# One inverse square root chain for each token tile of queries and keys, in place of four

## The chip, the cores and the metric

One core of a Trainium2 chip runs the whole program in one launch. The engines are named as in the profile: PE is TensorE (matmuls and transposes; PEld are its weight loads), DVE is VectorE, ACT is ScalarE, POOL is GpSimd, and SP issues most of the DMAs. The metric is the device time of the program in microseconds (us), lower being better; the median of several runs is given. All arithmetic is in float32, and a matmul of full precision is made of three products of high and low parts.

## The reference

The reference is one encoder layer over two sequences of 1024 and 256 tokens, taken here as 1280 tokens, or 10 tiles of 128. Only this part is touched: queries and keys of 8 heads are normalised head by head before the rotary embedding and the attention.

```python
q = (rms_norm(c_q, q_a_norm) @ w_uq).reshape(bsz, seq, N_HEADS, QK_HEAD)      # 96 per head
kv = (rms_norm(c_kv, kv_a_norm) @ w_ukv).reshape(bsz, seq, N_HEADS, QK_NOPE + V_HEAD)
k = jnp.concatenate([k_nope, k_rope], axis=-1)     # k_rope is shared by the heads
q = rms_norm(q, q_head_norm)       # x * rsqrt(mean(x*x) + EPS) * g, over the 96 of a head
k = rms_norm(k, k_head_norm)
...                                # rotary embedding on the last 32, then softmax attention
```

So each token has 8 inverse square roots for its queries and 8 for its keys. The rest of the layer (modulation, a convolution branch, a gated branch, three sigmoid gates, output products, a feed-forward block) is untouched.

## The kernel before

The program is one long list of jobs. 36 of them are products with a block of the input weights (`in_job`, 72 matmuls of `mm3` at L139 into a big PSUM tile); the last 24 of these make the gates (`gate`, L592 and L593: sigmoid on ACT, a store of 640 KB by SP). Smaller pieces of work wait in a list called `side`, and `run_side(n)` between two jobs takes n of them. Their instructions then stand in the program behind the gate just done and ahead of the next.

Queries and keys are such pieces (`prep_steps`). A token tile i has four units, in this order: queries of heads 0 to 3 (`q_unit`, tile psq), keys and values of heads 0 to 3 (`kv_unit`, tile pskv), then both for heads 4 to 7. One step makes one unit; four steps follow each of the gates 4 to 15, so that a gate and the four units of one tile make a turn. There are 40 units in 10 turns, and 12 turns have room for 48 steps.

A unit goes like this. PE makes the products (L510 or L535) into a PSUM tile. ACT squares them into a working slot `b_` (L513, L538). DVE sums the squares for each of 4 heads (L515, L540), scales the 4 sums (L516, L541), and runs `rsqrt_small` on the 4 columns: two integer instructions (L158, L159) and three rounds of three (L162 to L164), all on 128x4 tiles named zq or zk; a last instruction (L519, L544) folds in another factor. That is 13 small instructions a unit besides the sum. DVE also multiplies the products out of PSUM into `b_` (L524, three times, or L546), and POOL multiplies `b_` by the roots (L526 for queries, L550 and L548 for the two halves of the keys). For values ACT and DVE make a high and a low part (L555, L556), and SP stores them (L558).

`flip` comes LAG = 3 steps later: PE transposes the four heads of `b_` into a PSUM tile (L495), ACT copies it into a slot `o` (L497), DVE makes the low part (L498), and SP stores both halves, 256 KB each, to qk_d (L500). So step j issues unit j and then the flip of unit j - 3. The attention reads qk_d later, through POOL's queue.

Three resources are shared. psq, pskv and the transposes' tile pt take turns on two PSUM buffers (pool `sm`), so that each matmul of these kinds waits until the tile two before it has been read out. `b_`, `o`, the values' slot `vo`, the loaded latents and the gates take slots from one list of 33, of which the oldest free one is always used next; a slot that a DMA stores from is written again only when that DMA has landed. While the units run, 22 of the slots are held throughout (16 with the split activations h, 4 with split weights, 2 with tables). In the list as the program works it, 4 slots are free at the tightest place, and a slot is used again 5 to 7 takes after it was dropped. The weight blocks of a gate are split on POOL (L117, whi) and DVE (L120, wlo) one block at a time, when the buffers of an earlier block come free.

The order of each engine's instructions is fixed when the program is built, by a planner with costs of its own. It is not the order of the source: an instruction whose inputs are late by the plan steps behind later ones. So matmuls of the next gate stand between the matmuls of two units, and instructions of two units alternate on DVE. On the chip each engine keeps that order and waits where an input comes later than planned.

Of the kernel before, what the change touches and what calls it, by code (L numbers as in the profile page):

```python
# [11 lines left out]
F32 = mybir.dt.float32  # L12
# [3 lines left out]
ALU = mybir.AluOpType  # L16
AX = mybir.AxisListType
# [3 lines left out]
P = 128  # L21
# [6 lines left out]
EPS = 1e-6  # L28
# [6 lines left out]
LAG = 3  # L35
# [46 lines left out]
def build(tc, A):  # L82
# [6 lines left out]
    sm_p = enter(tc.tile_pool(name="smalls", bufs=4))  # L89
# [3 lines left out]
    V, S, G, PE, SY = nc.vector, nc.scalar, nc.gpsimd, nc.tensor, nc.sync  # L93
# [63 lines left out]
    def rsqrt_small(y, s, t):  # L157
        V.tensor_scalar(out=y.bitcast(I32), in0=s.bitcast(I32), scalar1=1, scalar2=None, op0=ALU.arith_shift_right)  # L158
        V.tensor_scalar(out=y.bitcast(I32), in0=y.bitcast(I32), scalar1=-1, scalar2=0x5F3759DF,  # L159
                        op0=ALU.mult, op1=ALU.add)  # L160
        for _ in range(3):
            V.scalar_tensor_tensor(out=t, in0=y, scalar=-0.5, in1=y, op0=ALU.mult, op1=ALU.mult)  # L162
            V.tensor_tensor(out=t, in0=t, in1=s, op=ALU.mult)
            V.scalar_tensor_tensor(out=y, in0=t, scalar=1.5, in1=y, op0=ALU.add, op1=ALU.mult)  # L164
# [25 lines left out]
    for k in range(KD):  # L190
# [3 lines left out]
        sq = sl.take()  # L194
# [3 lines left out]
    ps = big.tile([P, 1536], F32, name="pb", tag="pb")  # L198
# [5 lines left out]
    h = []  # L204
# [287 lines left out]
    def flip(src, which, i, g):  # L492
# [8 lines left out]
                         o[:, p * 512:(p + 1) * 512].bitcast(F32).rearrange("f (h t) -> f h t", h=4))  # L501
        sl.drop(o)

    def q_unit(i, g):
        ps = sm.tile([P, 512], F32, name="psq", tag="sm")
        for k in range(2):
            lh, ll = lat_of(i, k)
            wh, wl = kept[k]
            for q, (a, b) in enumerate(((lh, wh), (lh, wl), (ll, wh))):
                PE.matmul(ps[:, :384], a, b[:, g * 384:(g + 1) * 384], start=k == 0 and q == 0, stop=k == 1 and q == 2)  # L510
        b_ = sl.take()
        sq = b_[:, 512:896]
        S.activation(out=sq, in_=ps[:, :384], func=AF.Square)  # L513
        z = sm_p.tile([P, 4, 4], F32, name="zq", tag="z")
        V.tensor_reduce(out=z[:, 0, :], in_=sq.rearrange("p (h d) -> p h d", h=4), axis=AX.X, op=ALU.add)  # L515
        V.tensor_scalar(out=z[:, 0, :], in0=z[:, 0, :], scalar1=rr[:, 4, i:i + 1], scalar2=EPS,  # L516
                        op0=ALU.mult, op1=ALU.add)
        rsqrt_small(z[:, 1, :], z[:, 0, :], z[:, 2, :])
        V.tensor_scalar(out=z[:, 1, :], in0=z[:, 1, :], scalar1=rr[:, 2, i:i + 1], scalar2=96.0 ** -0.5,  # L519
                        op0=ALU.mult, op1=ALU.mult)  # L520
        qs = b_[:, :512].rearrange("p (h d) -> p h d", h=4)
        pv = ps[:, :384].rearrange("p (h d) -> p h d", h=4)
        for o, a, n in ((0, 0, 96), (96, 80, 16), (112, 64, 16)):
            V.tensor_tensor(out=qs[:, :, o:o + n], in0=pv[:, :, a:a + n],  # L524
                            in1=kept["cs"][:, i, o:o + n].unsqueeze(1).to_broadcast([P, 4, n]), op=ALU.mult)
        G.tensor_tensor(out=qs, in0=qs, in1=z[:, 1, :].unsqueeze(2).to_broadcast([P, 4, P]), op=ALU.mult)  # L526
        return b_, 0, i, g

    def kv_unit(i, g):
        gq, kr = kept["gq"], kept["kr"]  # L530
        ps = sm.tile([P, 512], F32, name="pskv", tag="sm")
        lh, ll = lat_of(i, 2)
        wh, wl = kept[g]
        for q, (a, b) in enumerate(((lh, wh), (lh, wl), (ll, wh))):
            PE.matmul(ps, a, b[:, 768:1280], start=q == 0, stop=q == 2)  # L535
        b_ = sl.take()
        sq = b_[:, 512:768]
        S.activation(out=sq, in_=ps[:, :256], func=AF.Square)  # L538
        z = sm_p.tile([P, 4, 4], F32, name="zk", tag="z")
        V.tensor_reduce(out=z[:, 0, :], in_=sq.rearrange("p (h d) -> p h d", h=4), axis=AX.X, op=ALU.add)  # L540
        V.tensor_scalar(out=z[:, 0, :], in0=z[:, 0, :], scalar1=rr[:, 5, i:i + 1], scalar2=rr[:, 6, i:i + 1],  # L541
                        op0=ALU.mult, op1=ALU.add)
        rsqrt_small(z[:, 1, :], z[:, 0, :], z[:, 2, :])
        V.tensor_scalar(out=z[:, 2, :], in0=z[:, 1, :], scalar1=rr[:, 3, i:i + 1], scalar2=None, op0=ALU.mult)  # L544
        ks = b_[:, :512].rearrange("p (h d) -> p h d", h=4)
        V.tensor_tensor(out=ks[:, :, 0:64], in0=ps[:, :256].rearrange("p (h d) -> p h d", h=4),  # L546
                        in1=gq[:, 96:160].unsqueeze(1).to_broadcast([P, 4, 64]), op=ALU.mult)
        G.tensor_tensor(out=ks[:, :, 0:64], in0=ks[:, :, 0:64],  # L548
                        in1=z[:, 2, :].unsqueeze(2).to_broadcast([P, 4, 64]), op=ALU.mult)
        G.tensor_tensor(out=ks[:, :, 64:128], in0=kr[:, i, :].unsqueeze(1).to_broadcast([P, 4, 64]),  # L550
                        in1=z[:, 1, :].unsqueeze(2).to_broadcast([P, 4, 64]), op=ALU.mult)
        vo = sl.take(F32R)
        vv = vo[:, :512].rearrange("p (h t d) -> p h t d", h=4, t=2)
        vp = ps[:, 256:512].rearrange("p (h d) -> p h d", h=4)
        S.activation(out=vv[:, :, 0, :], in_=vp, func=AF.Copy, scale=rr[:, 3, i:i + 1])  # L555
        V.scalar_tensor_tensor(out=vv[:, :, 1, :], in0=vp, scalar=rr[:, 3, i:i + 1],  # L556
                               in1=vv[:, :, 0, :].bitcast(F32), op0=ALU.mult, op1=ALU.subtract)
        SY.dma_start(v_d[g * 4:g * 4 + 4, :, i, :].rearrange("h p d -> p h d"),  # L558
                     vo[:, :512].bitcast(F32).rearrange("p (h d) -> p h d", h=4))
        sl.drop(vo)  # L560
        return b_, 1, i, g

    def prep_steps():
        units = [(i, g, f) for i in range(NT) for g in range(2) for f in (q_unit, kv_unit)]
        wait = []

        def step(j):
            if j < len(units):
                i, g, f = units[j]
                if (i, 0) == (0, g) and f is q_unit:  # L570
                    lat_get(0)
                if g == 0 and f is kv_unit and i + 1 < NT:
                    lat_get(i + 1)
                wait.append(f(i, g))
                if g == 1 and f is kv_unit:
                    sl.drop(kept.pop(("lat", i)))
            if j >= LAG:
                b_, which, i, g = wait.pop(0)
                flip(b_, which, i, g)
                sl.drop(b_)  # L580
            if j == len(units) + LAG - 1:
                for k in range(2):
                    sl.drop(*kept.pop(k))
                sl.drop(kept.pop("csg"), kept.pop("krr"))

        for j in range(len(units) + LAG):
            side.append(lambda j=j: step(j))

    def gate(br, m):
# [660 lines left out]
```

## Time and profile before

| | us |
|---|---|
| median of 3 runs | 2191.18 (2187.65 to 2191.96) |
| the profiled execution, its time | 2189.91 |
| the profiled execution, its span | 2188.1 |
| PE busy in the span | 2088.0 (95%) |
| DVE busy | 1541.6 (70%) |
| ACT busy | 750.9 (34%) |
| POOL busy | 688.7 (31%) |

The units' matmuls lie between 424.5 and 627 us from the start of the span, the flips between 433.8 and 640.6. The gates go on until 768 us, where the attention begins. A timeline row gives the start, the length, the engine, the line, the operation with what it writes and reads, and in brackets the engine's idle time ahead of it with what ended that. A busy PE is not PE at its peak, since ends of matmuls are modelled: successive matmuls overlap in the rows.

### The profile page before, as it was taken

Reading aid. Unit: us, or ns where it says so; the run is one execution under the profiler, and the core shown is the slowest. Engines: PE = TensorE matmul, PEld = TensorE weight load, DVE = VectorE, ACT = ScalarE, POOL = GpSimd, SP = SyncE. Lnnn points to the kernel's source line nnn. Section 1 sums busy time; section 2 is a strip of 40 time slices with the busy share of each in tenths; the row PEclk is TensorE's granted clock in tenths of the full one; section 3 lists DMA queues with packets and bytes.
Section 4 is the critical chain, followed back from the end, with each engine's and each line's share of the span. In section 5 each row is a group of like instructions: output and inputs, shape, how many; then the busy total and the mean of one; then the engine's idle time right before and its main releaser. Section 6 shows DMA issues by size and latency. Waiting matters only on the chain. (4 is left out here: it accounts for less than half of the span.)

```text
span 2188.1 us, 30072 instructions
## 1 busy us (share of the span) xinstructions
PE 2088.0 (95%) x11264; PEld 1791.5 (82%) x11264; DVE 1541.6 (70%) x2530; ACT 750.9 (34%) x1273; POOL 688.7 (31%) x541
## 2 busy tenths in 40 slices
PE   5899999999999999999999996999999999899999
PEld 5688888877778878888888875888888888688889
DVE  7696788778776778887796398766676666744344
ACT  5210031122322277763000155544444444322223
POOL 3401301322221234452043454444443444511000
PEclk9999999999999999999999998999999999999999
DMA  7301213366674723336635321223223232646455
GB/s 266 114 13 53 101 72 115 110 194 199 203 257 148 270 90 121 121 109 221 227 137 194 107 96 61 94 90 99 87 82 95 89 101 98 229 167 203 131 168 164
DMA packets 146546, 300.86 MB, mean 137 GB/s; under 512 B 12128, under 2 KB 69600, under 8 KB 146400
## 3 DMA queue, kind: packets, MB, share of 16 engines
q1 hardware_dynamic: 136032, 254.37, 34.6%
q0 software_dynamic: 10368, 44.57, 6.6%
q8 instruction: 89, 1.46, 0.3%
q14 instruction: 57, 0.47, 0.1%
HBM read 220.24 MB, written 78.64 MB: 137 GB/s over the span
## 5 line engine op out<-in xcount | busy, mean ns | idle before, releaser
L1033 PE MATMUL b<-t,wq 128*128 128x512 f32 (+1 forms) x2904 | 550.8, 352 | 18.9 <-ACT t L1055 13.1
L1033 PEld LDWEIGHTS b<-t,wq 128*128 128x128 f32 x2904 | 474.4, 190 | 95.7 <-ACT t L1055 13.6
L139 PE MATMUL pb<-t,whi 128*128 128x512 f32 (+1 forms) x1728 | 471.1, 358 | 8.1 <-DVE t L120 7.6
L120 DVE TENSOR_TENSOR wq<-wst,wq 128x512 fp32r<-128x512 f32 x308 | 252.2, 826 | 200.8 <-ACT wq L938 199.8
L139 PEld LDWEIGHTS pb<-t,whi 128*128 128x128 f32 x1728 | 307.1, 190 | 54.9 <-DVE t L120 9.3
L938 ACT ACTIVATE wq<-wst 128x512 fp32r<-128x512 f32 x308 | 193.1, 630 | 378.5 <-PE pd L1157 164.6
L1157 PE MATMUL pd<-t,wq 128*128 128x512 f32 (+1 forms) x1584 | 307.3, 356 | 10.4 <-ACT wq L938 5.0
L139 PE MATMUL pb<-t,wlo 128*128 128x512 f32 (+1 forms) x864 | 309.3, 358 | 1.6 <-DVE wlo L120 1.6
L1157 PEld LDWEIGHTS pd<-t,wq 128*128 128x128 f32 x1584 | 263.9, 191 | 53.8 <-ACT wq L938 5.4
L117 POOL TENSOR_SCALAR whi<-wst 128x1024 fp32r<-128x1024 f32 (+1 forms) x76 | 100.6, 1325 | 392.8 <-PE pb L139 207.1
L117 POOL TENSOR_SCALAR t<-t 128x512 fp32r<-128x512 f32 (+5 forms) x94 | 116.1, 1243 | 326.1 <-DMA t<-act_d 183.7
L139 PE MATMUL bp<-t,whi 128*128 128x512 f32 x640 | 198.9, 391 | 2.9 <-DVE t L120 2.9
L281 DVE SCALAR_TENSOR_TENSOR t<-t,col,t 128x1009 f32<-128x1009 f32 (+14 forms) x240 | 193.8, 871 | 0.0
L120 DVE TENSOR_TENSOR t<-t,t 128x512 fp32r<-128x512 f32 (+4 forms) x130 | 137.1, 1082 | 77.1 <-POOL t L117 76.2
L139 PEld LDWEIGHTS pb<-t,wlo 128*128 128x128 f32 x864 | 163.8, 190 | 23.5 <-DVE wlo L120 2.0
L120 DVE TENSOR_TENSOR wlo<-wst,whi 128x1024 fp32r<-128x1024 f32 (+1 forms) x76 | 86.0, 1134 | 98.5 <-POOL whi L117 63.1
L139 PEld LDWEIGHTS bp<-t,whi 128*128 128x128 f32 x640 | 118.1, 188 | 27.2 <-DVE t L120 4.1
L139 PE MATMUL bp<-t,wlo 128*128 128x512 f32 x320 | 124.5, 389 | 0.0
L693 POOL TENSOR_SCALAR t<-t,sz 128x1024 f32<-128x1024 f32 (+1 forms) x80 | 82.0, 1025 | 121.2 <-DVE sz L692 106.8
L685 PE MATMUL ps<-t,t 128*128 128x512 f32 (+1 forms) x432 | 114.5, 398 | 4.0 <-ACT t L691 2.5
L1091 POOL TENSOR_TENSOR t<-t,t 128x1280 f32<-128x1280 f32 x22 | 72.7, 3305 | 122.9 <-ACT wq L938 109.9
L592 ACT ACTIVATE t<-pb 128x1280 f32<-128x1280 f32 x24 | 29.8, 1242 | 209.6 <-PE pb L139 204.4
(199 smaller groups left out, 2902.1 us busy)
## 6 DMA issues: line engine op xcount, KB each, us to landing
wst<-in_wup SPq DMA_DIRECT2D x66, 512.0 KB, 3.6
wst<-in_wdn SPq DMA_DIRECT2D x132, 256.0 KB, 2.8
t<-in_ada SPq DMA_DIRECT2D x48, 512.0 KB, 5.7
qk_d<-t SPq DMA_DIRECT2D x80, 256.0 KB, 3.1
t<-qk_d POOLq DMA_DIRECT2D x32, 640.0 KB, 5.0
wst<-in_win SPq DMA_DIRECT2D x36, 512.0 KB, 3.8
gate_d<-t SPq DMA_DIRECT2D x24, 640.0 KB, 3.1
t<-gate_d SPq DMA_DIRECT2D x24, 640.0 KB, 5.5
```

The costliest lines, as they stand in the source:

```text
L117: G.tensor_scalar(out=out, in0=in_, scalar1=1.0, scalar2=0.0, op0=ALU.mult, op1=ALU.add)
L120: V.tensor_tensor(out=out, in0=in_, in1=hi.bitcast(F32), op=ALU.subtract)
L139: PE.matmul(ps.at(o, n) if isinstance(ps, Two) else ps[:, o:o + n], ws[:, c:c + P], ms[:, s:s + n], start=first and j == 0 and q == 0, sto ...
L281: V.scalar_tensor_tensor(out=ac[:, o + a:o + e], in0=ci[:, o + a + d:o + e + d], scalar=w, in1=ac[:, o + a:o + e], op0=ALU.mult, op1=ALU.add)
L592: S.activation(out=gt, in_=ps[:, :T], func=AF.Sigmoid)
L685: PE.matmul(ps[:, o + c:o + c + w], qk[a][:, q0:q0 + P], qk[b][:, k0 + c:k0 + c + w], start=q == 0, stop=q == 2)
L693: G.tensor_scalar(out=pr[:, o:o + n], in0=pr[:, o:o + n], scalar1=z[:, 2:3], scalar2=0.0, op0=ALU.mult, op1=ALU.add)
L938: S.activation(out=w[:, :HB], in_=src, func=AF.Copy)
L1033: PE.matmul(ps, w[:, c + k * P:c + (k + 1) * P], bs[k][i], start=start and k == 0 and q == 0, stop=stop and k == 3 and q == 2, skip_group_ ...
L1091: G.tensor_tensor(out=c["y1"], in0=c["y1"], in1=y2, op=ALU.mult)
L1157: PE.matmul(pss[m][:, :n], w[:, a + m * P:a + (m + 1) * P], t[:, b:b + n], start=k == 0 and q == 0, stop=k == KF - 1 and q == 2)
```

## The change

The 4 + 4 + 4 + 4 sums of a tile's four units go into one tile zt of 128x3x16. A unit now only squares, multiplies and sums. Behind the fourth unit, `scale_tile` scales the 16 sums with two instructions, runs `rsqrt_small` once on 16 columns, folds in the factors with two instructions, and then POOL multiplies all four units (six instructions). The flips wait for that: unit u of tile i, made in step 4i + u, is flipped in step 4i + u + 5 where it was 4i + u + 3. The last flip is in step 44, and step 45 drops the weights' slots. In `q_unit` the multiplications out of PSUM now stand ahead of the sum. With more `b_` slots held, 2 slots of the list are free at the tightest place, and most are used again 3 to 5 takes after they were dropped.

```diff
+    zt = {}
+
+    def sums(i, c, sq):
+        if c == 0:
+            zt[i] = sm_p.tile([P, 3, 16], F32, name="zt", tag="z")
+        V.tensor_reduce(out=zt[i][:, 0, c:c + 4], in_=sq.rearrange("p (h d) -> p h d", h=4), axis=AX.X, op=ALU.add)
+
     def q_unit(i, g):
...
         S.activation(out=sq, in_=ps[:, :384], func=AF.Square)
-        z = sm_p.tile([P, 4, 4], F32, name="zq", tag="z")
-        V.tensor_reduce(out=z[:, 0, :], in_=sq.rearrange("p (h d) -> p h d", h=4), axis=AX.X, op=ALU.add)
-        V.tensor_scalar(out=z[:, 0, :], in0=z[:, 0, :], scalar1=rr[:, 4, i:i + 1], scalar2=EPS,
-                        op0=ALU.mult, op1=ALU.add)
-        rsqrt_small(z[:, 1, :], z[:, 0, :], z[:, 2, :])
-        V.tensor_scalar(out=z[:, 1, :], in0=z[:, 1, :], scalar1=rr[:, 2, i:i + 1], scalar2=96.0 ** -0.5,
-                        op0=ALU.mult, op1=ALU.mult)
...
-        G.tensor_tensor(out=qs, in0=qs, in1=z[:, 1, :].unsqueeze(2).to_broadcast([P, 4, P]), op=ALU.mult)
+        sums(i, g * 8, sq)
         return b_, 0, i, g
 
     def kv_unit(i, g):
...
+        sums(i, g * 8 + 4, sq)
         SY.dma_start(v_d[g * 4:g * 4 + 4, :, i, :].rearrange("h p d -> p h d"),
...
+    def scale_tile(i, units):
+        z = zt.pop(i)
+        zs = [z[:, r, :].rearrange("p (g f h) -> p g f h", g=2, f=2) for r in range(3)]
+        V.tensor_scalar(out=zs[0][:, :, 0, :], in0=zs[0][:, :, 0, :], scalar1=rr[:, 4, i:i + 1], scalar2=EPS,
+                        op0=ALU.mult, op1=ALU.add)
+        V.tensor_scalar(out=zs[0][:, :, 1, :], in0=zs[0][:, :, 1, :], scalar1=rr[:, 5, i:i + 1],
+                        scalar2=rr[:, 6, i:i + 1], op0=ALU.mult, op1=ALU.add)
+        rsqrt_small(z[:, 1, :], z[:, 0, :], z[:, 2, :])
+        V.tensor_scalar(out=zs[2][:, :, 0, :], in0=zs[1][:, :, 0, :], scalar1=rr[:, 2, i:i + 1], scalar2=96.0 ** -0.5,
+                        op0=ALU.mult, op1=ALU.mult)
+        V.tensor_scalar(out=zs[2][:, :, 1, :], in0=zs[1][:, :, 1, :], scalar1=rr[:, 3, i:i + 1], scalar2=None,
+                        op0=ALU.mult)
+        for b_, f, _, g in units:
+            bs = b_[:, :512].rearrange("p (h d) -> p h d", h=4)
+            w = P if f == 0 else 64
+            G.tensor_tensor(out=bs[:, :, 0:w], in0=bs[:, :, 0:w],
+                            in1=zs[2][:, g, f, :].unsqueeze(2).to_broadcast([P, 4, w]), op=ALU.mult)
+            if f:
+                G.tensor_tensor(out=bs[:, :, 64:128], in0=kept["kr"][:, i, :].unsqueeze(1).to_broadcast([P, 4, 64]),
+                                in1=zs[1][:, g, 1, :].unsqueeze(2).to_broadcast([P, 4, 64]), op=ALU.mult)
...
                 if g == 1 and f is kv_unit:
                     sl.drop(kept.pop(("lat", i)))
-            if j >= LAG:
-                b_, which, i, g = wait.pop(0)
+                    scale_tile(i, wait)
+                    scaled.extend((j + 2, u) for u in wait)
+                    wait.clear()
+            if scaled and scaled[0][0] <= j:
+                b_, which, i, g = scaled.popleft()[1]
                 flip(b_, which, i, g)
                 sl.drop(b_)
```

## Rows read from the trace of the kernel before

**Rows 1.** Windows, turns 2 to 10: busy us (count) of PE, PEld, DVE, ACT, POOL.

```profile
442.85:634.00 191.15, 175.85 (x951) 147.14 (x950) 155.09 (x639) 58.94 (x103) 53.57 (x70) 1.00 0.67 204
```

**Rows 2.** Waits, 420 to 636 us: total us, times, longest.

```profile
PE pskv L535 <- DVE zq L162: 14.8, 9, 1.7
PEld pskv L535 <- issue: 22.4, 18, 2.1
```

**Rows 3.** Timeline of PE: first matmuls of two successive gates with no units between.

```profile
396.97 0.63 PE L139 MATMUL pb<-t,whi 128*128 128x512 f32 x2
...
410.75 0.63 PE L139 MATMUL pb<-t,whi 128*128 128x512 f32 x2
```

**Rows 4.** Timeline of PE: one turn, from its first unit to the next turn's.

```profile
506.93 1.21 PE L510 MATMUL psq<-t,t 128*128 128x384 f32 x6
...
510.92 0.93 PE L535 MATMUL pskv<-t,t 128*128 128x512 f32 x3
...
514.21 1.22 PE L510 MATMUL psq<-t,t 128*128 128x384 f32 x6
...
517.55 0.61 PE L139 MATMUL pb<-t,whi 128*128 128x512 f32 x2
519.83 0.94 PE L535 MATMUL pskv<-t,t 128*128 128x512 f32 x3 [1.66 <-DVE zq L162]
...
528.26 0.34 PE L510 MATMUL psq<-t,t 128*128 128x384 f32 x1
```

**Rows 5.** Timeline of DVE in the same turn.

```profile
508.15 1.23 DVE L120 TENSOR_TENSOR wlo<-wst,whi 128x1024 fp32r<-128x1024 f32 x1 [3.04 <-PE psq L510]
...
515.03 1.04 DVE L163 TENSOR_TENSOR zk<-zk 128x4 f32<-128x4 f32 x1
...
518.18 0.67 DVE L544 TENSOR_SCALAR zk<-zk,rr 128x4 f32<-128x4 f32 x1
...
518.83 0.21 DVE L524 TENSOR_TENSOR t<-psq,t 128x64 f32<-128x64 f32 x1
518.96 0.60 DVE L159 TENSOR_SCALAR zq<-zq 128x4 int32<-128x4 int32 x1
519.47 0.21 DVE L524 TENSOR_TENSOR t<-psq,t 128x64 f32<-128x64 f32 x1
```

**Rows 6.** Timeline of POOL in the same turn.

```profile
507.07 1.04 POOL L117 TENSOR_SCALAR whi<-wst 128x1024 fp32r<-128x1024 f32 x1 [0.34 <-PE pb L139]
515.02 1.04 POOL L526 TENSOR_TENSOR t<-t,zq 128x512 f32<-128x512 f32 x1 [6.90 <-DVE zk L162]
518.21 0.61 POOL L550 TENSOR_TENSOR t<-t,zk 128x256 f32<-128x256 f32 x1 [2.15 <-DVE zk L164]
```

**Rows 7.** Windows, turns 2 to 10, tile zk, then zq: busy us of DVE, POOL.

```profile
442.85:634.00 191.15, 66.19 (x252) 21.64 (x36) 1.00 0.67 204
...
442.85:634.00 191.15, 53.31 (x252) 18.74 (x18) 1.00 0.67 204
```

**Rows 8.** Tiles zq and zk: instructions by line, ns minimum/median/maximum, starts.

```profile
L515 DVE TENSOR_REDUCE zq<-t x20: 544/545/553, 426.9 to 623.5; 128x4 f32<-128x384 f32 x20
...
L163 DVE TENSOR_TENSOR zk<-zk x60: 145/163/1048, 430.9 to 632.3; 128x4 f32<-128x4 f32 x60
...
L540 DVE TENSOR_REDUCE zk<-t x20: 405/420/422, 428.4 to 627.7; 128x4 f32<-128x256 f32 x20
```

**Rows 9.** Tile qk_d, 424 to 640 us: landing of the stores of L500.

```profile
DMA to landing us min/median/max: 2.3/3.0/7.8
```

**Rows 10.** Timeline of ACT: copies of two flips in the turn of Rows 4.

```profile
512.61 0.60 ACT L497 ACTIVATE t<-pt 128x512 fp32r<-128x512 f32 x1 [0.34 <-PE pt L495]
...
515.95 0.60 ACT L497 ACTIVATE t<-pt 128x512 fp32r<-128x512 f32 x1
```

**Rows 11.** Timelines of DVE and ACT: end of side work, last gate's sigmoid.

```profile
751.88 0.23 DVE L614 TENSOR_SCALAR ada<-ada,col 128x2 f32<-128x2 f32 x1
...
766.56 1.24 ACT L592 ACTIVATE t<-pb 128x1280 f32<-128x1280 f32 x1 [12.53 <-PE pb L139]
```

More of the change, by code (lines that the diff above doesn't have):

```diff
@@ L525, in q_unit @@
                             in1=kept["cs"][:, i, o:o + n].unsqueeze(1).to_broadcast([P, 4, n]), op=ALU.mult)
-        G.tensor_tensor(out=qs, in0=qs, in1=z[:, 1, :].unsqueeze(2).to_broadcast([P, 4, P]), op=ALU.mult)
+        sums(i, g * 8, sq)
         return b_, 0, i, g
     def kv_unit(i, g):
-        gq, kr = kept["gq"], kept["kr"]
+        gq = kept["gq"]
         ps = sm.tile([P, 512], F32, name="pskv", tag="sm")
@@ L538, in kv_unit @@
         S.activation(out=sq, in_=ps[:, :256], func=AF.Square)
[L539 to L551, printed above, removed]
         vo = sl.take(F32R)
@@ L555, in kv_unit @@
         S.activation(out=vv[:, :, 0, :], in_=vp, func=AF.Copy, scale=rr[:, 3, i:i + 1])
+        ks = b_[:, :512].rearrange("p (h d) -> p h d", h=4)
+        V.tensor_tensor(out=ks[:, :, 0:64], in0=ps[:, :256].rearrange("p (h d) -> p h d", h=4),
+                        in1=gq[:, 96:160].unsqueeze(1).to_broadcast([P, 4, 64]), op=ALU.mult)
         V.scalar_tensor_tensor(out=vv[:, :, 1, :], in0=vp, scalar=rr[:, 3, i:i + 1],
                                in1=vv[:, :, 0, :].bitcast(F32), op0=ALU.mult, op1=ALU.subtract)
+        sums(i, g * 8 + 4, sq)
         SY.dma_start(v_d[g * 4:g * 4 + 4, :, i, :].rearrange("h p d -> p h d"),
@@ L561, in kv_unit @@
         return b_, 1, i, g
+    def scale_tile(i, units):
[18 more added lines that the diff above has]
+                                in1=zs[1][:, g, 1, :].unsqueeze(2).to_broadcast([P, 4, 64]), op=ALU.mult)
     def prep_steps():
         units = [(i, g, f) for i in range(NT) for g in range(2) for f in (q_unit, kv_unit)]
-        wait = []
+        wait, scaled = [], deque()
+        last = len(units) + LAG + 2
         def step(j):
@@ L576, in step @@
                     sl.drop(kept.pop(("lat", i)))
-            if j >= LAG:
-                b_, which, i, g = wait.pop(0)
+                    scale_tile(i, wait)
[3 more added lines that the diff above has]
+                b_, which, i, g = scaled.popleft()[1]
                 flip(b_, which, i, g)
                 sl.drop(b_)
-            if j == len(units) + LAG - 1:
+            if j == last:
                 for k in range(2):
@@ L584, in step @@
                 sl.drop(kept.pop("csg"), kept.pop("krr"))
-        for j in range(len(units) + LAG):
+        for j in range(last + 1):
             side.append(lambda j=j: step(j))
```

## The prediction

> **What bounds the kernel now.** I read the busy times by stretch first, then the waits of TensorE, then the timelines of one turn (a gate and the four units behind it). Queries and keys fill 191 us, the turns of tiles 1 to 9. In them PE is busy 175.85 us, DVE 155.09, ACT 58.94, POOL 53.57, and the granted clock is 1.00, so PE runs at its upper level throughout [rows 1]. PE is the bound, DVE the next behind it. The list of waits shows one wait of PE of any size there: the keys' products wait 14.8 us for DVE, 9 times, 1.7 at the longest, which is once a turn and 1.65 us each [rows 2]. A gate alone takes 410.75 - 396.97 = 13.78 us [rows 3]; a turn takes 528.26 - 506.93 = 21.33 us [rows 4]; four units and four flips so cost 7.55 us with that stall in them.
>
> The timeline says which of the two key units it is. The first pskv starts at 510.92 with no wait noted. The second psq starts at 514.21, gate products fill PE until 518, and the second pskv starts at 519.83 behind 1.66 us of idleness [rows 4]. It needs the PSUM buffer of that psq, which DVE frees with its last multiplication at 519.47, for 0.21 us [rows 5]: 0.15 us later PE goes on. So the question is why DVE is late. In rows 5 three tiny instructions of the chains, each of 4 columns, are long: 1.04, 0.67 and 0.60 us, where the median of such a one is 0.163 and the longest 1.048 [rows 5, 8]. The first two lie beside a multiplication of POOL, from start to end (515.02 for 1.04, 518.21 for 0.61) [rows 6]. Over 0.163 they are 0.88 + 0.51 + 0.44 = 1.8 us long together, about the stall. The planner's order fits chains that don't meet POOL; on the chip they do, and the multiplications that free PSUM stand behind them on DVE.
>
> **The change part by part.**
>
> *Chains.* DVE spends 66.19 + 53.31 = 119.50 us on the tiles of the chains in 9 turns, the sums of squares among it [rows 7]. The sums stay: 18 x 0.545 + 18 x 0.420 = 17.4 us [rows 8]. So 102.1 us, or 11.3 us a tile, is 52 small instructions with their collisions. In their place come 15 on 16 or 8 columns. The trace has none of that width; between 0.163 us for 4 columns [rows 8] and 0.21 for 64 out of PSUM [rows 5] 15 of them cost 2.4 to 3.2 us, and I take 2.7. DVE sheds some 8.6 us of its 155.09 / 9 = 17.2 a turn. By itself this is worth nothing, since DVE is not the bound: PE's products lie over it.
>
> *The stall.* What counts is that no chain stands any more between a unit's square and the multiplications that free its PSUM tile. In the second half of a turn DVE has, from the square on, three multiplications of psq, the sum, and a flip's low part. Without the chain instructions of the other unit the buffer is free well ahead of 518, where PE has arrived, so the 1.65 us should go: 9 x 1.65 = 14.8 us. The weight loads of pskv stand idle 22.4 us in 18 waits [rows 2], two a turn; that holds the same stall, the smaller gaps ahead of the first pskv, and what a change of operand takes in any case. It is the upper bound: 22.4 us. The lower bound is below nothing, as the rivals show. I take 15.5, the stall and a third of a microsecond in all for what else is late at the first pskv, since the wait of PE itself is the row nearest to it.
>
> *What is late next.* With pskv on time PE is the bound of the turn without a wait: 21.33 - 1.7 = 19.6 us, against DVE at 17.2 - 8.6 = 8.6 and POOL at 53.57 / 9 = 6.0.
>
> *POOL.* Its multiplications stay six a tile: (21.64 + 18.74) / 9 = 4.5 us [rows 7]. They are now one block behind the chain, where they were four pieces. They meet no chain then. The block's cover is the rest of the gate's products, 528.26 - 519.83 = 8.4 us less the unit and its flip [rows 4]. Behind the block on POOL stands the split of a weight block (1.04 us at 507.07) [rows 6], and behind that DVE's wlo (1.23 us at 508.15) [rows 5]; that weight block is for a later gate. This is where the change may take something back (first rival).
>
> In sentences of their own: the Trainium skill (SBUF — State Buffer, "Who interferes with whom") has it that a DVE instruction with two SBUF inputs, or in a two-port mode, and a POOL instruction reading SBUF lock each other out for a whole instruction. The rows of 1.04 beside 1.04 and 0.67 beside 0.61 agree. By that rule the block can still cost DVE its wlo, once a turn by at most one POOL instruction, 1.04 us.
>
> *Flips.* They come two steps later, so all wait for a POOL that finished a gate earlier; their 40 transposes, copies, low parts and 80 stores are the same. SP issues each later, past a gate's store and a weight load, which are ready at that point and cost nothing. The last flip comes after gate 15 in place of 14, about 20 us later by PE. Nothing reads it until the attention, whose way is set by the side work behind the gates: that ends at 751.88, against the last gate's sigmoid at 766.56 [rows 11], 14.7 us of cover. If the side work starts a gate late (13.8 us) it just fits; without that cover each microsecond more is lost whole.
>
> *Slots.* Two are free at the tightest place, four before. So the copy of a flip now waits, in half of the cases, for the landing of a store issued one step ahead. The landing takes 3.0 us, 2.3 to 7.8 [rows 9], and the copy before it 0.60 [rows 10]: 3.6 us at least from one copy to the next, where two lie 515.95 - 512.61 = 3.34 us apart now [rows 10]. That is a new wait on ACT. What stands behind it there are squares, and behind these PE's next unit. Its cost lies between 0, as gate products can be placed between, and the second rival. I take 0.
>
> **The sum.** The profiled execution took 2189.91 us, 1.8 over its span. Less 15.5 it is 2174.4. It lies 1.3 under the median of the runs, so on the median 2191.18 - 15.5 = 2175.7 us.
>
> **The rivals.**
>
> 1. *The block takes the place of the stall.* POOL's 4.5 us come behind pskv's sum and a chain of some 2.7 us. If the block ends 2 us into the next turn, whi and wlo are late by that, and if wlo stands ahead of psq's multiplications on DVE, the first pskv waits for it. For it: wlo does stand at the head of the turn now (508.15, while psq is done by then) [rows 4, 5]. Against it: the planner knows POOL's lengths and can put wlo behind. A lateness of 0.9 us leaves 0.75 x 9 = 6.8 us of gain: 2184. One of 1.65 or more leaves nothing: 2191.
>
> 2. *The slots make it slower.* One link of copy, store and landing a turn that takes 0.6 + 5.4 us (a landing midway between 3.0 and 7.8) in place of 3.34 is 2.7 us late [rows 9, 10]. Where PE's order has no gate product for that time, PE loses 2.7 and regains 1.65: 9 x 1.05 = 9.5 us, 2200.7. It decides from a lateness of 1.65 a turn. For it: only 2 slots are left. Against it: ACT is busy 58.94 of 191 us and 13.78 us of gate products a turn can be put in between [rows 1, 3].
>
> 3. *The change doesn't do what it says.* DVE's time is off the path and the stall comes from the order of the two PSUM buffers alone. Then a wait of the same size stays: 2191. Against it: the long instructions add up to the stall.
>
> **How the numbers follow.** Forecast (11 to 22 us gained): 0.57. First rival with part of the gain (4.4 to 11): 0.18. Nothing gained, by the first or third: 0.12. Slots, or a planner's order that turns out worse elsewhere: 0.13. What a measurement of this kernel can tell from no change is about 0.2%, or 4.4 us. So faster 0.75, the same 0.12, slower 0.13. The range goes from 2191.18 - 22.4 less 1.5 for the spread of runs, 2167, to 2191; above it lie the slower cases and half of the unchanged ones, some 0.19.
>
> **What would show it.** Right: no wait of PE at pskv over 0.5 us in turns 2 to 10; a turn of 19.3 to 19.9 us; DVE busy in these turns some 77 us less; no instruction of the chains as long as a POOL multiplication, except by wlo; the gates ending, and the attention starting, about 15 us sooner. First rival: a wait at the first pskv of a turn with wlo ahead of it on DVE. Second: ACT waiting for stores of qk_d ahead of L497 or L538. The forecast is wrong if PE's idle time at L535 stays over 8 us, or if it goes and the time after the gates doesn't follow.

## The result and the profile after

The changed kernel takes 2204.15 us (median of 6 runs, 2198.78 to 2209.58) against 2190.24 for the kernel before (6 runs, 2187.65 to 2195.62). The ratio is 1.0061, with a 95% interval of 1.0046 to 1.0076: slower by some 13.9 us, where 15.5 us less were forecast. The profiled execution took 2203.46 us, its span is 2201.6. The busy line of its page:

```profile
PE 2096.9 (95%) x11264; PEld 1801.0 (82%) x11264; DVE 1484.9 (67%) x2160; ACT 753.2 (34%) x1275; POOL 690.6 (31%) x541
```

DVE did shed work (1541.6 before). The matmuls are the same in number and PE's busy time is 8.9 us longer, so some of them ran slower. The attention starts at 783.4 in place of 767.9, 15.5 us late, and the span is 13.5 longer: the loss arises before the attention, in the turns. Their windows, answering to [rows 1], with the same columns (busy us and count of PE, PEld, DVE, ACT, POOL, then the granted clock, the DMA share and GB/s): first turns 2 to 10, which take 205 us where they took 191, then two single microseconds within one turn.

```profile
441.00:646.00 205.00, 185.34 (x948) 155.74 (x947) 103.82 (x305) 55.60 (x101) 52.03 (x70) 0.94 0.61 185
...
603.00:604.00 1.00, 0.49 (x1) 0.50 (x2) 1.00 (x5) 0.00 (x0) 0.00 (x0) 0.50 0.59 81
...
610.00:611.00 1.00, 1.00 (x6) 0.90 (x6) 0.00 (x0) 0.39 (x2) 0.00 (x0) 1.00 0.00 0
```

The mean clock is 0.94 where it was 1.00: in some stretches the granted clock is 0.50, which is the lower level (1.2 GHz). The waits from 424 to 680 us (total, times, longest), answering to [rows 2]:

```profile
DVE wlo L120 <- POOL whi L117: 65.3, 11, 10.1
...
PE pskv L535 <- DVE t L524: 19.6, 8, 3.9
...
ACT t L497 <- DMA qk_d<-t: 12.6, 7, 3.5
...
ACT t L538 <- DMA qk_d<-t: 7.7, 7, 1.3
```

PE waits at the same line as before, L535, but longer: 19.6 us in 8 waits. It is now the first pskv of a turn, not the second, and what frees the PSUM buffer late is again L524. ACT waits 20.3 us for stores of qk_d, of which the trace before had none. One turn shows how these belong together. First PE (start, length, operation, in brackets the idle time ahead and what ended it), answering to [rows 4]:

```profile
586.88 0.95 PE L535 MATMUL pskv<-t,t 128*128 128x512 f32 x3
...
595.92 1.21 PE L517 MATMUL psq<-t,t 128*128 128x384 f32 x6
596.97 0.60 PE L495 MATMUL pt<-ident,t 128*128 128x128 f32 x4
...
599.25 0.39 PE L139 MATMUL pb<-t,wlo 128*128 128x512 f32 x1
603.51 1.62 PE L535 MATMUL pskv<-t,t 128*128 128x512 f32 x3 [3.87 <-DVE t L524]
```

DVE in the same turn, answering to [rows 5]:

```profile
591.67 0.18 DVE L162 SCALAR_TENSOR_TENSOR zt<-zt 128x16 f32<-128x16 f32 x1
593.65 0.69 DVE L498 TENSOR_TENSOR t<-pt,t 128x512 fp32r<-128x512 f32 x1 [1.80 <-ACT t L497]
...
595.43 0.62 DVE L564 TENSOR_SCALAR zt<-zt,rr 128x8 f32<-128x8 f32 x1
601.41 1.23 DVE L120 TENSOR_TENSOR wlo<-wst,whi 128x1024 fp32r<-128x1024 f32 x1 [5.36 <-POOL whi L117]
602.55 0.81 DVE L524 TENSOR_TENSOR t<-psq,t 128x384 f32<-128x384 f32 x3
```

POOL, answering to [rows 6], and ACT, answering to [rows 10]:

```profile
595.40 1.19 POOL L572 TENSOR_TENSOR t<-t,zt 128x256 f32<-128x256 f32 x2 [19.01 <-DVE zt L164]
596.55 3.19 POOL L569 TENSOR_TENSOR t<-t,zt 128x512 f32<-128x512 f32 x4
599.68 0.60 POOL L485 DMA_DIRECT2D t<-lat_d  x1
600.32 1.06 POOL L117 TENSOR_SCALAR whi<-wst 128x1024 fp32r<-128x1024 f32 x1
```

```profile
588.78 0.38 ACT L538 ACTIVATE t<-pskv 128x256 f32<-128x256 f32 x1 [0.97 <-DMA qk_d<-t]
...
593.01 0.60 ACT L497 ACTIVATE t<-pt 128x512 fp32r<-128x512 f32 x1 [3.48 <-DMA qk_d<-t]
596.18 1.24 ACT L608 ACTIVATE t<-pb 128x1280 f32<-128x1280 f32 x1 [2.56 <-PE pb L139]
```

Read from the end. The first pskv starts at 603.51, when DVE's multiplications out of psq (602.55 for 0.81) have freed its buffer; psq itself was done by 597.1. They stand behind wlo (601.41), wlo needs whi (600.32), and whi stands on POOL behind the block of six multiplications, which ran from 595.40 to 599.74, and the issue of a load (599.68). The block waited for the end of the chain, and two waits for stores make the chain late: ACT's square of the turn's last unit waited 0.97 us (588.78), and the chain stood still for 1.80 us behind a low part (593.65) whose copy on ACT waited 3.48 us (593.01). The last unit itself (586.88) also stands late in PE's order, as e11 will show. The gate's sigmoid stands at 596.18, so nearly the whole block falls into the next turn. PE keeps its order, in which that pskv is next, and idles from 599.64.

That gap costs more than itself. PE was idle for 3.87 us; the clock then was 0.50 from 603 to 609 while PE worked, and the same pskv took 1.62 us where it took 0.93 and 0.94 before [rows 4]. Over one-microsecond windows from 424 to 664 us, the parts of the clock that were not granted add up to 11.95 us, in six such stretches, each behind a wait at pskv of 2.1 us or more; behind the waits of 1.66 us before there was none. Waits 4.8 us longer and 11.95 us of clock make 16.8, less 0.8 by which the units' stage begins sooner (sigmoid of the gate ahead of it at 423.94 against 424.78): 16.0, against the 15.5 by which the attention starts late.

### The profile page after: what moved, and what is told of

Read it like the earlier page. It is cut to its first block, busy times and chain, and to the rows that moved or that the text cites. A ratio compares the mean times of both kernels' runs of the same rounds, so it can differ in the third digit from the quotient of the medians.

```text
span 2201.6 us, 29740 instructions
## 1 busy us (share of the span) xinstructions
PE 2096.9 (95%) x11264; PEld 1801.0 (82%) x11264; DVE 1484.9 (67%) x2160; ACT 753.2 (34%) x1275; POOL 690.6 (31%) x541
## 5 line engine op out<-in xcount | busy, mean ns | idle before, releaser
L139 PE MATMUL pb<-t,whi 128*128 128x512 f32 (+1 forms) x1728 | 476.2, 361 | 8.4 <-DVE t L120 8.0
L139 PEld LDWEIGHTS pb<-t,whi 128*128 128x128 f32 x1728 | 311.0, 192 | 56.6 <-DVE t L120 9.4
L139 PE MATMUL pb<-t,wlo 128*128 128x512 f32 (+1 forms) x864 | 311.3, 360 | 1.6 <-DVE wlo L120 1.6
L139 PE MATMUL bp<-t,whi 128*128 128x512 f32 x640 | 198.9, 391 | 2.9 <-DVE t L120 2.9
L139 PEld LDWEIGHTS pb<-t,wlo 128*128 128x128 f32 x864 | 165.4, 191 | 23.9 <-DVE wlo L120 2.0
L139 PEld LDWEIGHTS bp<-t,whi 128*128 128x128 f32 x640 | 118.1, 188 | 27.3 <-DVE t L120 4.1
L139 PE MATMUL bp<-t,wlo 128*128 128x512 f32 x320 | 124.5, 389 | 0.0
L706 DVE TENSOR_REDUCE sz<-ps 128x1 f32<-128x1024 f32 (+1 forms) x80 | 84.4, 1060 | 16.3 <-PE ps L701 12.7
```

The source lines that it names most:

```text
L139: PE.matmul(ps.at(o, n) if isinstance(ps, Two) else ps[:, o:o + n], ws[:, c:c + P], ms[:, s:s + n], start=first and j == 0 and q == 0, sto ...
L706: V.tensor_reduce(out=z[:, 0:1], in_=ps[:, o:o + n], axis=AX.X, op=ALU.max, negate=True)
```

## The experiments

Each was timed beside the kernel before on the same chip, and ratios are to that, with 95% intervals. The questions in turn were: is it the slots or POOL's block; was the stall before rightly read; and why are some variants slow without any wait.

**e1_lag5.** The kernel before with its flips two steps later, so that slots are taken and given back as in the changed one, but with chains and POOL's work in four pieces.

```diff
-LAG = 3
+LAG = 5
```

> The kernel before with its flips five steps behind their units, where they were three: the list of slots is then used take for take as in the changed kernel (2 free at the tightest place), and the four chains and POOL's four separate pieces stay. Theory A (the block of POOL's six multiplications holds up whi, whi holds up wlo, and psq's multiplications stand behind wlo on DVE, so PE waits at the first pskv of a turn and its clock falls): the stall of 1.65 us a turn at the second pskv stays, none of over 0.5 us appears at the first, the granted clock stays 1.00, and the time is that of before within 4 us (2186 to 2195). Theory B (too few free slots: copies of flips wait for stores of qk_d, DVE waits for the copies, PE for DVE): ACT waits some 20 us for qk_d in the turns as in the changed kernel, and the time is some 13 us longer, 2200 to 2207.

2195.4 us, ratio 1.0013 (1.0000 to 1.0025), about 3 us slower.

```profile
PE pt L495 <- DVE zq L516: 4.3, 7, 1.0
PE pskv L535 <- DVE zq L162: 2.8, 2, 1.4
PE pskv L535 <- DVE zq L159: 2.5, 3, 1.1
...
ACT t L497 <- DMA qk_d<-t: 11.9, 11, 2.3
```

ACT's new wait for stores is there, a little over half as long; PE's waits are short, 10.1 us in all, and the clock stays 1.00. At pskv 5.3 us are left, where Theory A had the whole old stall stay, and the flips wait 4.3. The attention starts at 767.3 against 767.9 before, so the 3 us are lost behind it and not in the turns. With waits of this size the slots alone do not make the loss.

**e2_whi_act.** The changed kernel, with the high parts of the gates' weights made by ACT, so that nothing that PE needs soon stands behind POOL's block.

```diff
-        to_hi(hi[:, :n], st[:, :n])
+        if act:
+            S.activation(out=hi[:, :n], in_=st[:, :n], func=AF.Copy)
+        else:
+            to_hi(hi[:, :n], st[:, :n])
...
-        job(fn, (A["win"][b],))
+        job(fn, (A["win"][b], D, b >= 12))
```

> The changed kernel with the high part of a gate's weight block made on ACT, where POOL made it: DVE's wlo no longer stands behind POOL's block. Slots as in the changed kernel. Theory A: the wait at the first pskv of a turn (19.6 us in 8) is gone or under 5 us in all, the granted clock in the turns is 1.00, and the time falls by some 25 us against the changed kernel, to 2174 to 2184. Theory B: waits of ACT for qk_d stay, and with them the waits of PE and the time, 2198 to 2207.

2191.32 us, ratio 0.9994 (0.9982 to 1.0005): the loss is gone, 12.8 us less than the changed kernel, and no gain is left.

```profile
PE psq L520 <- DVE t L549: 3.3, 5, 1.0
PE pt L498 <- DVE t L501: 3.2, 2, 1.9
PE pt L498 <- DVE zt L560: 2.8, 2, 2.6
ACT t L500 <- DMA qk_d<-t: 26.6, 13, 3.9
```

The wait at pskv is gone, so the way from block to whi to wlo to psq is confirmed. ACT now waits even longer for the stores, and PE waits 9.3 us elsewhere, at flips above all. Behind two of these waits, of 2.65 and 1.93 us, the clock is 0.50 again, and the parts not granted add up to 3.4 us. The time lies between the ranges of the two theories: the block carried the loss to PE, but was not its only source.

**e3_before_whi_act.** The same edit in the kernel before, as control.

```diff
...
-        job(fn, (A["win"][b],))
+        job(fn, (A["win"][b], D, b >= 12))
```

> The control: the kernel before with the same move of the gates' high parts to ACT. Theory A: it takes nothing from the stall at the second pskv, which comes from chains that meet POOL's pieces; the time is that of before within 4 us. Theory B: the same. If it is faster by over 8 us, the gain of the move is not the block's.

2191.53 us, ratio 0.9998 (0.9988 to 1.0009), with 14.1 us of waits at pskv as before. Moving whi is worth nothing by itself; what e2 gained back is the block's.

**e4_half, e5_half_again.** The changed kernel with one chain of 8 columns for each two units, hence two blocks of half the length a turn, and flips three steps behind their unit, as before. e5 is the same kernel again, without an edit.

```diff
-            zt[i] = sm_p.tile([P, 3, 16], F32, name="zt", tag="z")
+            zt[i] = sm_p.tile([P, 3, 8], F32, name="zt", tag="z")
...
-        last = len(units) + LAG + 2
+        last = len(units) + LAG
...
+                if f is kv_unit:
                     scale_tile(i, wait)
```

> The changed kernel with a chain of 8 columns for each two units (one group of four heads), so twice a tile, POOL's block in two of 2.2 us, and the flips three steps behind their units: slots take for take as in the kernel before. Theory A: the second block still ends in the next turn's beginning but 2 us sooner; the wait at the first pskv is under 1 us a turn, the clock stays 1.00, and the time is 2174 to 2186. Theory B: the waits for qk_d are gone, and the time is 2174 to 2186 too; e1 and e2 tell A from B, this one says whether both can be had at once.

> The kernel with two chains of 8 columns a tile once more. In its first profile every 512 column matmul of the program came 1.4% slower than in the other kernels, also in stages whose instructions are the same and at a granted clock of 1.00, so its 2208.8 us say little of the turns. If that belongs to the program, it is 2205 to 2211 again with 395 ns for such a matmul; if it belonged to that load of it, matmuls are at 390 ns and, by Theory A and by Theory B, it takes 2174 to 2190.

2208.79 us, ratio 1.0078 (1.0062 to 1.0093), and again 2210.23, ratio 1.0074 (1.0055 to 1.0092). A miss: it is the slowest so far although its trace has no wait at pskv, 7.8 us of waits in all at the flips (pt, 6.8 of them behind POOL) and a clock of 1.00. The matmuls themselves are slower, in all stages: 395 ns for 512 columns in the feed-forward block, far behind the turns, against 390 before. As it came again, it belongs to the program, and e9 and e10 look for its cause.

**e6_half_whi_act.** e4 with the edit of e2 besides.

```diff
...
-        job(fn, (A["win"][b],))
+        job(fn, (A["win"][b], D, b >= 12))
```

> Two chains of 8 columns a tile (slots as in the kernel before) and the gates' high parts on ACT: neither the block ahead of whi nor the lack of slots is left. Theory A and B together: no wait of PE over 1 us in the turns, under 5 us in all, clock 1.00, turns of 19.3 to 20.2 us, and 2172 to 2184 us. If it is not under 2187, something else than these two takes the gain.

2204.86 us, ratio 1.0059 (1.0044 to 1.0074). A miss too: it has the slow pace, so it says little about whi.

**e7_whi_act_due1.** e2 with the flips one step sooner as well: one more slot is free at the tightest place (3), and slots are used again after 4 to 6 takes.

```diff
-        last = len(units) + LAG + 2
+        last = len(units) + LAG + 1
...
-                    scaled.extend((j + 2, u) for u in wait)
+                    scaled.extend((j + 1, u) for u in wait)
```

> The changed kernel with the gates' high parts on ACT, and each flip one step sooner: 3 slots free at the tightest place, used again after 4 to 6 takes. Against e2, which has 2191.3 us, 9.3 us of waits of PE and 26.6 us of waits of ACT's flip copies for qk_d. Theory B (what is left in e2 comes from the slots): waits for qk_d fall under 12 us, those of PE under 5 us, the clock in the turns is 1.00, and it takes 2177 to 2186 us. Theory A alone (the slots cost nothing): as e2, 2188 to 2194.

2178.67 us, ratio 0.9939 (0.9924 to 0.9954). Now the forecast's turn is there: eight turns of 19.49 us lie between these two sigmoids of gates, where 19.6 was named as PE's bound without a wait.

```profile
441.24 1.22 ACT L611 ACTIVATE t<-pb 128x1280 f32<-128x1280 f32 x1
...
597.15 1.22 ACT L611 ACTIVATE t<-pb 128x1280 f32<-128x1280 f32 x1
```

A window of it (PE busy 179.99 of 180 us):

```profile
440.00:620.00 180.00, 179.99 (x980) 152.60 (x980) 105.69 (x307) 68.81 (x115) 43.12 (x61) 1.00 0.75 222
```

The attention starts at 749.9, 18 us sooner, of which the next stage gives 5 back: from the first bp product to the first of b it takes 289.9 us where it took 284.9. e1 shows the same there (289.8). That was not followed up.

**e8_products_first.** The kernel before, with the multiplications out of PSUM and the values' parts put ahead of the sum and the chain in each unit; four chains a tile, as before.

```diff
         S.activation(out=sq, in_=ps[:, :384], func=AF.Square)
+        for o, a, n in ((0, 0, 96), (96, 80, 16), (112, 64, 16)):
+            V.tensor_tensor(out=qs[:, :, o:o + n], in0=pv[:, :, a:a + n],
...
         z = sm_p.tile([P, 4, 4], F32, name="zq", tag="z")
...
```

> One part of the change alone: the kernel before with the multiplications that free PSUM (and the values' two parts) ahead of the sum and the chain in each unit; four chains of 4 columns, POOL's pieces, slots and flips as before. If the stall at the second pskv comes from the place of the multiplications behind the chain on DVE, it goes here too: waits of PE at pskv under 5 us in all (14.8 before) and 2174 to 2184 us. If it comes from the time of the chains, it stays, and the time is 2187 to 2194.

2181.93 us, ratio 0.9955 (0.9939 to 0.9971).

```profile
PE pt L495 <- DVE zk L164: 3.7, 8, 0.5
```

The stall at pskv is gone with all chains in place, and turns take 20.26 us (442.69 to 604.75, eight of them). So the stall was rightly read: chains standing ahead of the instructions that free PSUM, not DVE's load.

**e9_half_pad.** e4, with its tile padded to the 192 bytes a partition that the changed kernel's has, so that all that lies behind it is at the same place again.

```diff
-            zt[i] = sm_p.tile([P, 3, 8], F32, name="zt", tag="z")
+            zt[i] = sm_p.tile([P, 6, 8], F32, name="zt", tag="z")
```

> Two chains of 8 columns a tile as in e4, whose matmuls of 512 columns are 1.3% slower everywhere (395 to 397 ns against 390 to 392). Its small tiles take 128 bytes a partition more than before's, and the slots lie behind them in memory; here the tile is made as large as the changed kernel's. Theory C (the address of the slots against that of the weights sets the matmuls' pace): they are back at 390 to 392 ns, and the time falls to 2178 to 2190, the turns to 20.4 us or less. If the pace is something else's, 2204 to 2213 as e4 and e5.

2183.02 us, ratio 0.9960 (0.9945 to 0.9975): 25.8 us less than e4, by the padding alone, and the matmuls are back at 390 ns. Its turns take 20.6 us, just over the 20.4 expected.

**e10_before_shift.** The same test on the kernel before: its chains' tiles get 32 bytes that nothing uses, which moves the slots 128 bytes on in each partition. No instruction is added, and the order on every engine is the same.

```diff
-        z = sm_p.tile([P, 4, 4], F32, name="zq", tag="z")
+        z = sm_p.tile([P, 6, 4], F32, name="zq", tag="z")
...
-        z = sm_p.tile([P, 4, 4], F32, name="zk", tag="z")
+        z = sm_p.tile([P, 6, 4], F32, name="zk", tag="z")
```

> The kernel before with nothing changed but the size of the chains' tile, 128x6x4 where 128x4x4 is used, so that the slots lie 128 bytes a partition further on; every engine's instructions and their order are the same. Theory C: matmuls of 512 columns at 395 to 397 ns and 2205 to 2215 us. Otherwise 2187 to 2195.

2213.65 us, ratio 1.0099 (1.0080 to 1.0118). Groups of matmuls from 1400 to 1800 us (busy us, mean ns, idle before), in the kernel before and then in e10:

```profile
L1033 PE MATMUL b<-t,wq 128*128 128x512 f32 x1357 | 313.8, 390 | 0.0
...
L1033 PE MATMUL b<-t,wq 128*128 128x256 f32 x768 | 97.1, 283 | 0.0
```

```profile
L1033 PE MATMUL b<-t,wq 128*128 128x512 f32 x1329 | 314.3, 395 | 0.0
...
L1033 PE MATMUL b<-t,wq 128*128 128x256 f32 x768 | 96.6, 282 | 0.0
```

Each matmul of 512 columns in this group takes 5 ns more, those of 256 columns do not, and the waits at pskv are 14.4 us where they were 14.8. The pace hangs on where the tiles lie. The changed kernel has 390 ns in this window, so its own loss is not of this kind.

**e11_due1.** The changed kernel with nothing but the flips one step sooner; whi stays on POOL behind the same block.

```diff
-        last = len(units) + LAG + 2
+        last = len(units) + LAG + 1
...
-                    scaled.extend((j + 2, u) for u in wait)
+                    scaled.extend((j + 1, u) for u in wait)
```

> The changed kernel with each flip one step sooner, so with 3 slots free at the tightest place and later reuse; the gates' high parts stay on POOL, behind the block. It is the fourth corner to the changed kernel (2204), e2 (2191.3) and e7 (2178.7). Theory A (whi and wlo behind the block are a cause by themselves): waits of PE at the first pskv of a turn stay over 10 us in all, and it takes 2188 to 2200. Theory B (they matter only because late stores make the chain late): they go, and it takes 2178 to 2186.

2180.21 us, ratio 0.9947 (0.9930 to 0.9964): 24 us less than the changed kernel. First a window, then the waits for stores, then timelines of POOL and of ACT (the gate's sigmoid) in one turn:

```profile
440.00:620.00 180.00, 179.06 (x969) 149.67 (x968) 103.12 (x306) 55.53 (x101) 52.57 (x70) 1.00 0.72 216
```

```profile
ACT t L520 <- DMA qk_d<-t: 1.0, 1, 1.0
ACT t L497 <- DMA qk_d<-t: 0.5, 1, 0.5
```

```profile
595.51 1.18 POOL L572 TENSOR_TENSOR t<-t,zt 128x256 f32<-128x256 f32 x2 [13.97 <-DVE zt L164]
596.65 3.18 POOL L569 TENSOR_TENSOR t<-t,zt 128x512 f32<-128x512 f32 x4
600.24 1.05 POOL L117 TENSOR_SCALAR whi<-wst 128x1024 fp32r<-128x1024 f32 x1 [0.41 <-PE pb L139]
```

```profile
600.31 1.25 ACT L608 ACTIVATE t<-pb 128x1280 f32<-128x1280 f32 x1 [7.78 <-PE pb L139]
```

The block is as long as in the changed kernel, but it ends before the gate does, and POOL then idles until the gate gives the weights' buffers free. There is no wait at pskv at all, and ACT's wait for stores fell from 20.3 to 1.5 us. The theory by which the block alone holds up the turn is refuted.

The planner's order, which neither theory named, differs too. In PE's timeline (the last pskv of the turn, the first psq of the next):

```profile
589.61 0.96 PE L535 MATMUL pskv<-t,t 128*128 128x512 f32 x3
...
600.11 1.21 PE L517 MATMUL psq<-t,t 128*128 128x384 f32 x6
```

Here 52 of a gate's 72 products stand between these two, 10.5 us; in the changed kernel it is 45, 9.0 us (586.88 to 595.92). So chain and block have 1.5 us more cover by the order alone.

**e12_half_pad_whi_act.** e9 with whi on ACT.

```diff
...
-        job(fn, (A["win"][b],))
+        job(fn, (A["win"][b], D, b >= 12))
```

> e9 with the gates' high parts on ACT. Theory A: the shorter blocks of e9 hold up whi little, and this gains 0 to 8 us over it, 2174 to 2186; both beat the kernel before. If it is at 2188 or above, two chains a tile have a cost of their own.

2180.25 us, ratio 0.9946 (0.9926 to 0.9965), with 6.4 us of waits left at the flips. Where the chain is in time, whi's engine matters little (e9: 2183.02).

**e13_due1_hold.** e11 moved the flips and with them freed a slot; either could be the cure. Here one slot is held back, so that 2 are free as in the changed kernel, with the flips where e11 has them.

```diff
+        held = sl.take()
...
             if j == last:
+                sl.drop(held)
```

> e11 (each flip one step sooner, 2180.2 us) with one slot held back while the units run, so that 2 are free at the tightest place and are used again after 3 to 5 takes, as in the changed kernel. Theory B (the slots: copies wait for stores, which makes chain and block late): waits of ACT for qk_d over 10 us and of PE at the first pskv over 8 us come back, the granted clock falls in some turns, and it takes 2190 to 2206. Theory D (the place of the flips in the turn): as e11, 2178 to 2184.

2213.53 us, ratio 1.0094 (1.0068 to 1.0121).

```profile
PE pskv L535 <- DVE t L524: 20.2, 8, 3.1
ACT t L497 <- DMA qk_d<-t: 18.9, 9, 3.4
...
ACT t L538 <- DMA qk_d<-t: 8.9, 8, 1.3
```

One slot fewer brings back all of it: 20.2 us of waits at pskv, the waits for stores, a clock of 0.95. So it is the number of free slots, not the step of the flips. PE's order is again that of the changed kernel, with 45 products behind the last pskv: the slots act through the planner's order as well as through the waits for stores, and no run separates the two. The time came out above what was expected. Its profiled execution, the shortest of four at 2206.29 us, loses its time in the turns as the changed kernel does (last gate's sigmoid at 783.39); where the longer ones lose 7 to 9 more, no trace shows (their mean granted clock is 0.980 to 0.982, against 0.983).

**e14_short_block.** The other half of the question: the slots as in the changed kernel, POOL's block short. The four multiplications in place (of queries and of the first halves of keys by their roots) are left out, so these stay unscaled; the block is 1.2 us.

```diff
-            w = P if f == 0 else 64
-            G.tensor_tensor(out=bs[:, :, 0:w], in0=bs[:, :, 0:w],
-                            in1=zs[2][:, g, f, :].unsqueeze(2).to_broadcast([P, 4, w]), op=ALU.mult)
```

> The changed kernel without the four multiplications in place on POOL (queries and the first halves of the keys stay unscaled); the two for the keys' second halves stay, so the block is 1.2 us long where it was 4.4, and whi stays behind it on POOL. Slots as in the changed kernel. Theory A (the block holds up whi, wlo and psq's multiplications): waits of PE at the first pskv fall under 6 us in all, and the time is 2180 to 2194, as e2 or below. Theory B alone (late stores would do it without the block): 2198 to 2207.

2188.17 us, ratio 0.9983 (0.9970 to 0.9996).

```profile
ACT t L497 <- DMA qk_d<-t: 17.3, 12, 3.1
ACT t L538 <- DMA qk_d<-t: 10.2, 7, 3.1
...
PE pskv L535 <- DVE t L524: 2.6, 3, 1.9
```

ACT waits 27.5 us for stores, more than in the changed kernel, PE's order is the same as there, and yet pskv waits 2.6 us only and the clock is 1.00. The profiled execution is the shortest of ten (2183.24). The block is needed for the loss as well.

Put together, in us, for the changed kernel and its variants with a full chain (2190 to 2192 before):

| | 2 slots free | 3 slots free |
|---|---|---|
| whi behind the block on POOL | 2204.15 (e13: 2213.53) | 2180.21 |
| whi on ACT | 2191.32 | 2178.67 |

One slot more is worth 23.9 us with whi behind the block and 12.7 without; moving whi is worth 12.8 us with 2 slots and 1.5 with 3. The slots are the larger cause. Neither alone makes the kernel slower than before, but the slots alone take away all of the gain (e2) or most of it (e14).

## Why the prediction was wrong

- *The bound and the stall.* Right. PE is the bound, and e8 shows that the stall of 1.65 us came from chains ahead of the multiplications that free PSUM. In the changed kernel no wait is left at the second pskv.
- *Chains.* Right in size. On the tile zt DVE is busy 45.81 us from 441 to 646 us where it was 119.50 on zk and zq [rows 7]: 8.2 us a turn less, forecast 8.6. The rounds on 16 columns take 0.17 to 0.18 us each; 15 instructions at 2.7 were taken. DVE's whole busy time in these windows fell by 51.3 us, not 77, to 11.5 a turn where 8.6 was named; in the rows before the small instructions overlap others, and the busy time of an engine counts that once.
- *No long chain instruction but by wlo.* Nearly. The one row that is long is L564, 0.62 us beside the block's first multiplication (0.60), where the like L562 takes 0.23. Lines of tile zt (ns minimum/median/maximum, starts), answering to [rows 8]:

```profile
L163 DVE TENSOR_TENSOR zt<-zt x30: 165/174/177, 432.2 to 641.4; 128x16 f32<-128x16 f32 x30
...
L562 DVE TENSOR_SCALAR zt<-zt,rr x10: 230/231/232, 433.9 to 641.8; 128x8 f32<-128x8 f32 x10
L564 DVE TENSOR_SCALAR zt<-zt,rr x10: 593/615/617, 434.0 to 642.0; 128x8 f32<-128x8 f32 x10
```

  By the Trainium skill (SBUF — State Buffer, "Who interferes with whom") a DVE and a POOL instruction that both need the pair of ports they share lock each other out for a whole instruction. The trace agrees (0.62 beside 0.60), but in L564 and not in wlo, which I had named and which keeps its 1.23 us. It costs nothing here.
- *What is late next.* The number was right, 19.6 us, and e7 (19.49) reaches it. What was wrong is that nothing would come ahead of PE.
- *Slots: "I take 0".* This step failed. The term put at 0 measures 23.9 us (2204.15 against 2180.21 in e11, with one slot more), and 12.7 with whi off POOL (e2 against e7). The copies and squares wait 20.3 us for stores. The landing was of the size I read (2.6 us, 2.3 to 7.6, against [rows 9]); the error is that I looked for the cost only at PE's next unit, and priced the two rivals apart. ACT's wait reaches PE by another way: it makes the last square and the chain late, and the chain's end starts POOL's block. Besides, with 2 slots the planner leaves 1.5 us less cover behind the last unit, which I did not look for.
- *POOL: the block's cover.* The cover of 8.4 us assumed a chain that ends soon after its unit. In e11 it does, and the block ends as the gate does; in the changed kernel the block starts 0.8 us before the gate's sigmoid and runs into the next turn. The place was the first rival's, with wlo ahead of psq's multiplications as it feared; its trigger was the second's. Against the kernel before, either alone costs nothing in the turns (e1, e2 and e14 with the slots short; e11 with the block), so the chances, which took them as separate cases, were wrong together.
- *The size.* The first rival ended at no gain, since I let a late block only take the old stall's place. Its waits are longer than the old ones (2.1 to 3.9 us at most turns, against 1.66), and then the clock falls, which I had not priced: 11.95 of the 16.8 us. The second rival's 2200.7 lies near the result, but by a sum that the trace doesn't show.
- *Flips.* Right: the last gate's sigmoid and the attention's start are both 15.5 us later, so the late flips cost nothing of their own.

What stays open: how much of the slots' cost is the planner's order and how much the waits for stores, the pace of the matmuls by address (below), the 5 us that e1 and e7 lose after the attention, and the longer executions of e13. Five variants that compute the same beat both kernels; e7 (2178.67), e11 (2180.21) and e12 (2180.25) are within their spreads of each other, and e11 is the changed kernel but for the step at which its flips are due.

## What to carry to other kernels

A change that holds buffers of a shared list longer has to be priced by how many takes later a buffer is used again, against the landing of its store, and the wait followed along every queue behind it to the engine that sets the time, not only to the next instruction; the order that a planner chooses for fewer buffers is part of that price. Small pieces that are gathered into one block on an in-order engine must end before what stands behind them is needed; free PSUM first, ahead of any chain of small instructions, as e8 does with the old chains. And keep the tiles at the same addresses when two layouts are compared.

## What the runs showed of the hardware

- *Addresses.* Moving the slots by 128 bytes a partition, with the same instructions in the same order, made matmuls of 512 columns with a weights' tile take 395 ns where they took 390 (L1033; 396 against 391 at L139 into bp) and the program 22 us longer (2213.65, ratio 1.0099), and padding took 25.8 us off e4. Those between slots and slots did not change (389 ns at L354 before and in e10), so it is the place of the slots against the weights' tiles that seems to matter. That is an inference from the groups; which part of the address decides was not tried.
- *The clock.* Of the waits of PE in the turns of the changed kernel, six of 2.1 to 3.9 us were followed by some microseconds at a granted clock of 0.50, one of 2.09 was not, and neither were those of 1.66 us before. In e2 one of 1.93 us was, in e13 one of 2.18 was not: the length of the wait alone does not decide it. PE was at work again while the clock was low; so the six waits, 16.7 us together by themselves, cost 11.95 us more.
